# Sliding windows scattered from SBUF: whole first tiles of two neighbouring columns in place of half-filled ones

**Chip, cores, metric.** One core of a Trainium2 chip. The metric is the device time of one execution in microseconds, as a median over runs of the state "fast" (within 1.5% of the fastest run of the same kernel).

## The reference

```python
def setup_inputs():
    batch, c, h, w = (16, 64, 64, 64)          # float32, window 8, stride 4
def reference(x, window_size, stride):
    n_h = n_w = 15
    for i in range(n_h):
        for j in range(n_w):
            result[:, i, j] = x[:, :, 4*i:4*i+8, 4*j:4*j+8].copy()
```

Nothing is computed. 16.78 MB are read, each pixel goes into up to four windows, and 58.98 MB are written: 16 x 15 x 15 = 3600 output rows of 64 x 8 x 8 floats, 16 KB each.

## The kernel before

The input lies once in SBUF, as `L[128, 32, 16, 64]`. A partition is (channel half, batch, quarter of the height): 2 x 16 x 4. A store takes a tile `G[128, 64, 8, 8]`, one whole output row in each partition, and scatters it by a list of row numbers. ScalarE (ACT) and VectorE (DVE) copy the windows from `L` into one of four such tiles, GpSimd (POOL) issues the scatter. Rows whose number lies out of bounds (`FAR` is added) are skipped.

```python
    # loads: lower channels on SyncE's queue (28 of 32 channels) and POOL's (4), upper channels on POOL's
    for y in range(NY):                 # NY = 2 batch halves
        for q in range(HQ):             # HQ = 4 quarters of the height
            hw = y * HQ + q < HWP
            if hw:
                load(nc.sync, 0, y, q, SMALL, CL)
            load(nc.gpsimd, 0, y, q, 0, SMALL if hw else CL)
            load(nc.gpsimd, 1, y, q, 0, CL)
    # ... cut: fill() copies windows of 64 or 32 partitions from L into G
    EARLY = NG - 1                      # NG = 4 tiles
    zero = ipool.tile([P, 1], f32, name="zero")
    nc.vector.memset(zero[:, :], 0.0)
    for g in G:
        act(out=g.rearrange("p c r w -> p (c r w)"), in_=zero.to_broadcast([P, CFREE]))

    def part(y, j):                     # one column of one batch half: 64 of 128 rows, the others skipped
        g = tile_()
        for half in range(CH):
            fill(g, half, half, j, y * QP, QP, (dve, dve) if y and half else (act, dve))
        scatter(g, (idx_y0, idx_y1)[y], j, 0)

    def unit(j, s):
        g = tile_()
        if s == 0:                      # "plain": 128 rows, two ACT and two DVE copies
            for half in range(CH):
                fill(g, half, half, j, 0, HP, (act, dve))
            scatter(g, idx, j, s)
        else:                           # "crossed": 112 rows; 16 of one half are skipped, turn says which
            turn = int(crossed % 5 in (1, 3))
            crossed += 1
            fill(g, turn, s, j, 0, HP, (act, act))
            fill(g, 1 - turn, s + 1, j, 0, HP, (dve, dve))   # copy, and a stream shuffle for the lower rows
            scatter(g, (idx_hi, idx_lo)[turn], j, s)

    for j in range(EARLY):
        part(0, j)
    # ... cut: three times part(1, j) and a plain tile; then two crossed tiles and a plain one, and so on
    # the last column: two tiles, four stores each, on SyncE's queue
            free(nc.sync.dma_start(out=o_q[q * NSLOT + s, j], in_=g_q[QP + q : QP + q + (B - 1) * HQ + 1 : HQ]))
```

Parts exist because the first half of the batch is in SBUF long before the second (ACT's copies from the first half start at 29.52 us, the next ones, from the second, at 47.91): storing can be prepared while loads still run.

## Time and profile before

| | before |
|---|---|
| time, median | 194.81 us (194.69 to 195.04) |
| span in the profile | 192.9 us |
| DMA moved | 75.81 MB |
| busy: ACT, DVE, POOL | 72%, 57%, 28% |

How to read it: the bytes are fixed by the task, so the time is bytes over the rate of the DMA engines (420 GB/s from 58 to 180 us), plus every stretch in which those engines wait.

### The profile page before, as it was taken

Reading aid. Unit: us, or ns where it says so; the run is one execution under the profiler, and the core shown is the slowest. Engines: PE = TensorE matmul, PEld = TensorE weight load, DVE = VectorE, ACT = ScalarE, POOL = GpSimd, SP = SyncE. Lnnn points to the kernel's source line nnn. Section 1 sums busy time; section 2 is a strip of 40 time slices with the busy share of each in tenths; the row PEclk is TensorE's granted clock in tenths of the full one; section 3 lists DMA queues with packets and bytes.
Section 4 is the critical chain, followed back from the end, with each engine's and each line's share of the span. In section 5 each row is a group of like instructions: output and inputs, shape, how many; then the busy total and the mean of one; then the engine's idle time right before and its main releaser. Section 6 shows DMA issues by size and latency. Waiting matters only on the chain.

```text
span 192.9 us, 487 instructions
## 1 busy us (share of the span) xinstructions
DVE 110.2 (57%) x153; ACT 138.3 (72%) x70; POOL 54.6 (28%) x53
## 2 busy tenths in 40 slices
DVE  5000007700999979876876875874974794723330
ACT  8993008940897879999778777877977797754560
POOL 7402212531166430422214123134043124320000
DMA  2999999999989999999999999999999999999764
GB/s 79 337 404 400 399 401 397 401 401 407 421 357 418 404 423 421 425 421 404 426 425 428 420 411 418 432 435 411 404 435 418 425 431 404 418 432 435 321 292 177
DMA packets 11588, 75.81 MB, mean 393 GB/s; under 512 B 3888, under 2 KB 3888, under 8 KB 7984
## 3 DMA queue, kind: packets, MB, share of 16 engines
q0 software_dynamic: 9472, 66.34, 83.8%
q1 hardware_dynamic: 2112, 9.44, 12.4%
q14 instruction: 4, 0.03, 0.0%
HBM read 16.78 MB, written 69.21 MB: 446 GB/s over the span
## 4 chain that ended last, share of the span: by engine, by line
DMA 73%; DVE 12%; issue 7%; POOL 2%; ACTq 1%; ACT 1%; DVEq 0%; PEldq 0%
DMA out_dram<-G,idx 34%; DMA out_dram<-G,idx_hi 22%; DMA L<-in_x_dram 16%; DVE G L144 9%; POOL L L58 2%; DVE G L146 2%; DVE G L147 2%; ACTq L245 1%; ACT G L211 1%; DVEq L144 0%; POOL pi L69 0%; DVEq L146 0%; PEldq L245 0%; ACTq L211 0%
## 5 line engine op out<-in xcount | busy, mean ns | idle before, releaser
L144 ACT COPY G<-L 64x2048 f32<-64x2048 f32 (+1 forms) x61 | 115.3, 1896 | 40.0 <-issue 20.7
L144 DVE COPY G<-L 64x2048 f32<-64x2048 f32 (+1 forms) x37 | 45.0, 1224 | 41.9 <-DMA L<-in_x_dram 27.1
L147 DVE STREAM_SHUFFLE G<-L 64x1024 f32<-64x1024 f32 x30 | 38.3, 1277 | 0.0
L146 DVE COPY G<-L 64x1024 f32<-64x1024 f32 x30 | 21.6, 720 | 21.5 <-DMA out_dram<-G,idx 16.2
L124 POOL DMA_INDIRECT out_dram<-G,idx_hi x9 | 12.0, 1338 | 34.9 <-DVE G L147 24.5
L58 POOL DMA_DIRECT2D L<-in_x_dram x16 | 11.4, 715 | 23.9 <-DMA L<-in_x_dram 23.4
L124 POOL DMA_INDIRECT out_dram<-G,idx x11 | 12.4, 1126 | 18.6 <-ACT G L144 15.9
L124 POOL DMA_INDIRECT out_dram<-G,idx_lo x6 | 8.9, 1480 | 24.1 <-DVE G L147 17.0
L124 POOL DMA_INDIRECT out_dram<-G,idx_y x6 | 9.6, 1603 | 16.0 <-ACT G L144 8.9
L157 ACT COPY G<-zero 128x4096 f32<-128x4096 f32 x4 | 14.1, 3600 | 0.0
L211 ACT COPY G<-L 32x2048 f32<-32x2048 f32 x4 | 7.6, 1896 | 7.4 <-DMA out_dram<-G,idx 4.9
L211 DVE COPY G<-L 32x2048 f32<-32x2048 f32 x4 | 4.9, 1220 | 10.1 <-DMA out_dram<-G,idx 6.6
L157 ACT ACT_TABLE_LOAD x1 | 1.3, 1283 | 0.7 <-PEq L231 0.7
L155 DVE MEMSET zero<- 128x1 f32 x1 | 0.1, 59 | 0.8 <-PEq L231 0.8
L78 DVE CUSTOM_DVE_ANT_0 idx_y<-idx,th 128x2 uint16<-128x2 uint16 x2 | 0.3, 160 | 0.1
L78 DVE TENSOR_TENSOR th<-tc,tq 128x1 int32<-128x1 int32 x2 | 0.3, 158 | 0.1
L75 DVE TENSOR_SCALAR th<-tc 128x1 int32<-128x1 int32 x2 | 0.3, 154 | 0.0
L69 POOL IOTA pi<- 128x1 int32 x1 | 0.1, 125 | 0.4 <-PEq L245 0.4
L72 DVE TENSOR_SCALAR tb<-pi 128x1 int32<-128x1 int32 x1 | 0.2, 154 | 0.1
L147 DVE LOAD_MASK_SELECT G<-L x30 | 0.2, 6 | 0.0
L78 DVE CUSTOM_DVE_ANT_0 idx_hi<-idx,th 128x2 uint16<-128x2 uint16 x1 | 0.2, 160 | 0.0
L78 DVE CUSTOM_DVE_ANT_0 idx<-tb,th 128x2 uint16<-128x2 uint16 x1 | 0.2, 159 | 0.0
(16 smaller groups left out, 2.2 us busy)
## 6 DMA issues: line engine op xcount, KB each, us to landing
L<-in_x_dram POOLq DMA_DIRECT2D x8, 1024.0 KB, 21.0
L<-in_x_dram SPq DMA_DIRECT2D x8, 896.0 KB
out_dram<-G SPq DMA_DIRECT2D x8, 256.0 KB
L<-in_x_dram POOLq DMA_DIRECT2D x8, 128.0 KB, 21.1
out_dram<-G,idx POOLq DMA_INDIRECT x11, 14.5
out_dram<-G,idx_hi POOLq DMA_INDIRECT x9, 14.1
out_dram<-G,idx_y POOLq DMA_INDIRECT x6, 9.8
out_dram<-G,idx_lo POOLq DMA_INDIRECT x6, 12.9
```

The lines of the kernel that those rows point to most:

```text
L58: eng.dma_start(out=L[p0 : p0 + QP - HQ + 1 : HQ, c0:c1, :, :], in_=x_v[ch, y, q, :, c0:c1, :])
L69: nc.gpsimd.iota(pi[:, :], pattern=[[0, 1]], base=0, channel_multiplier=1)
L72: nc.vector.tensor_scalar(out=d[:, :], in0=pi[:, :], scalar1=shift, scalar2=mask, op0=ALU.logical_shift_right, op1=ALU.bitwise_and)
L75: nc.vector.tensor_scalar(out=d[:, :], in0=a[:, :], scalar1=float(m), scalar2=None, op0=ALU.mult)
L78: nc.vector.tensor_tensor(out=d[:, :], in0=a[:, :], in1=b[:, :], op=op)
L124: st = nc.gpsimd.indirect_dma_start(out=o_v, out_offset=bass.IndirectOffsetOnAxis(ap=ix[:, 0:1], axis=0), in_=g.rearrange("p c r w -> p (c ...
L144: copy(out=g[d, cs, :, :], in_=L[f, :, s * ST : s * ST + WS, cols])
L146: copy(out=g[d, cs, 0:ST, :], in_=L[f, :, s * ST : RB, cols])
L147: nc.vector.stream_shuffle(out=g[d, cs, ST:WS, :], in_=L[f, :, 0:ST, cols], mask=nxt)
L157: act(out=g.rearrange("p c r w -> p (c r w)"), in_=zero.to_broadcast([P, CFREE]))
L211: copy(out=g[d, ch * CL : (ch + 1) * CL, :, :], in_=L[f, :, s * ST : s * ST + WS, cols])
L245: with _tile.TileContext(nc) as tc:
```

## The change

Its intent: a part takes columns j and j + 1 of one batch half, so that all 128 rows are real; three plain tiles fewer are needed; no tile has unwritten rows, so the zeroing goes; the 16 skipped rows of the crossed tiles alternate between the halves; the last stores are issued on two queues. (The loads, four channels in each small one, are as they were.)

```diff
-    EARLY = NG - 1
-    zero = ipool.tile([P, 1], f32, name="zero")
-    nc.vector.memset(zero[:, :], 0.0)
-    for g in G:
-        act(out=g.rearrange("p c r w -> p (c r w)"), in_=zero.to_broadcast([P, CFREE]))
+    EARLY = 3
@@ def part(y, j):
-        for half in range(CH):
-            fill(g, half, half, j, y * QP, QP, (dve, dve) if y and half else (act, dve))
+        for d in range(P // QP):
+            s, dj = d // NY, d % NY
+            cols = slice((j + dj) * ST, (j + dj) * ST + WS)
+            for ch in range(CH):
+                f = (ch * NY + y) * QP
+                (act, dve)[(d + ch) % 2](
+                    out=g[d * QP : (d + 1) * QP, ch * CL : (ch + 1) * CL, :, :],
+                    in_=L[f : f + QP, :, s * ST : s * ST + WS, cols],
+                )
@@ def unit(j, s):
-            turn = int(crossed % 5 in (1, 3))
+            turn = crossed % 2
@@ order of the tiles
-        part(0, j)
+        part(0, 2 * n)
-    plain = [(j, 0) for j in range(EARLY, NW - 1)]
+    plain = [(j, 0) for j in range(2 * EARLY, NW - 1)]
-        for w in cross[:2]:
+        for w in cross[:3]:
@@ last column
-            free(nc.sync.dma_start(...))
+            free((nc.sync, nc.scalar)[s * q % 2].dma_start(...))
```

(Cut: the row numbers for the parts, which put the second column in place of the skipped rows.)

More of the change, by code (lines that the diff above doesn't have):

```diff
@@ L89 @@
     bits(th, 5, 1)
-    mul(th, th, FAR)
-    tt(idx_y0, idx, th, ALU.add)
-    nc.vector.tensor_scalar(out=th[:, :], in0=th[:, :], scalar1=-1.0, scalar2=FAR, op0=ALU.mult, op1=ALU.add)
-    tt(idx_y1, idx, th, ALU.add)
+    mul(idx_y0, th, 1 - YB * NWIN)
+    tt(idx_y0, idx_y0, idx, ALU.add)
+    nc.vector.tensor_scalar(out=idx_y1[:, :], in0=idx_y0[:, :], scalar1=float(YB * NWIN), scalar2=None, op0=ALU.add)
     nc.vector.tensor_scalar(out=tq[:, :], in0=tq[:, :], scalar1=float(HQ - 1), scalar2=FAR, op0=ALU.is_equal, op1=ALU.mult)
@@ L186, in unit @@
             scatter(g, (idx_hi, idx_lo)[turn], j, s)
-    for j in range(EARLY):
-        part(0, j)
-    plain = [(j, 0) for j in range(EARLY, NW - 1)]
+    for n in range(EARLY):
+        part(0, 2 * n)
+    plain = [(j, 0) for j in range(2 * EARLY, NW - 1)]
     cross = [(j, 2) for j in range(NW)]
-    for j in range(EARLY):
-        part(1, j)
+    for n in range(EARLY):
+        part(1, 2 * n)
         unit(*plain.pop(0))
     while plain:
-        for w in cross[:2]:
+        for w in cross[:3]:
             unit(*w)
-        cross = cross[2:]
+        cross = cross[3:]
         unit(*plain.pop(0))
@@ L213 @@
         for q in range(HQ):
-            free(nc.sync.dma_start(out=o_q[q * NSLOT + s, j], in_=g_q[QP + q : QP + q + (B - 1) * HQ + 1 : HQ]))
+            free((nc.sync, nc.scalar)[s * q % 2].dma_start(out=o_q[q * NSLOT + s, j], in_=g_q[QP + q : QP + q + (B - 1) * HQ + 1 : HQ]))
 _INS = ['x', 'window_size', 'stride']
```

## The prediction

> **What bounds the kernel now.** I read the page first: engine shares, the 40 slices, the DMA queues and the chain. Then I cut the span into windows at the dips of the DMA row, and read the timelines of ACT and POOL around each dip.
>
> ```profile
> DVE 110.2 (57%) x153; ACT 138.3 (72%) x70; POOL 54.6 (28%) x53
> ...
> DMA  2999999999989999999999999999999999999764
> ...
> DMA packets 11588, 75.81 MB, mean 393 GB/s; under 512 B 3888, under 2 KB 3888, under 8 KB 7984
> ...
> q0 software_dynamic: 9472, 66.34, 83.8%
> ...
> HBM read 16.78 MB, written 69.21 MB: 446 GB/s over the span
> ...
> DMA 73%; DVE 12%; issue 7%; POOL 2%; ACTq 1%; ACT 1%; DVEq 0%; PEldq 0%
> ```
>
> The 16 DMA engines are the bound: 9 in nearly every slice, 73% of the chain. 75.81 MB is exactly the input (16.78 MB) plus the output (58.98 MB) plus instructions. So **skipped rows move nothing**. The HBM line hides this: its 69.21 MB is the output plus 10.22 MB, which is 624 rows of 16 KB, just the number skipped (6 part stores x 64, 15 crossed stores x 16). That counter seems to count them; the packets do not: q0's 66.34 MB is 9.44 MB of loads and 3472 real rows. The packet records have 4-byte packets of about 9 ns in the skipped rows' places.
>
> ```profile
> core 0: us, DVE busy (x) ACT busy (x) POOL busy (x), PEclk, DMA share, GB/s
> ...
> 46.00:48.00 2.00, 0.02 (x1) 0.10 (x1) 0.00 (x0) 1.00 1.17 441
> 48.00:54.00 6.00, 5.88 (x5) 5.51 (x3) 1.52 (x1) 1.00 1.00 421
> 54.00:56.00 2.00, 1.94 (x3) 1.98 (x2) 1.36 (x2) 1.00 0.67 271
> 56.00:58.00 2.00, 1.94 (x3) 1.95 (x3) 0.84 (x1) 1.00 0.95 393
> 58.00:180.00 122.00, 88.10 (x115) 98.42 (x52) 35.17 (x27) 1.00 1.01 420
> 180.00:184.00 4.00, 1.39 (x2) 1.59 (x2) 0.00 (x0) 1.00 0.68 285
> 184.00:188.00 4.00, 1.05 (x1) 2.36 (x2) 0.00 (x0) 1.00 0.72 303
> 188.00:193.00 5.00, 0.00 (x0) 0.00 (x0) 0.00 (x0) 1.00 0.44 184
> ```
>
> From 48 to 54 us the stores in flight are part stores with half their rows skipped, and yet real bytes move at 421 GB/s, as later (420). From 420 GB/s over 16 engines, one 16 KB row costs an engine 0.624 us; a full store (8 rows an engine) 4.99 us, a crossed one on average 4.37 us. What is not full: the start; a dip at 54 to 58 us worth about 0.33 x 2 + 0.05 x 2 = 0.8 us; and the tail from 180 us, where the share is 0.7.
>
> ```profile
> 0.74 1.28 ACT L157 ACT_TABLE_LOAD   x1 [0.74 <-PEq L231]
> ...
> 29.52 11.01 ACT L144 COPY G<-L 32x2048 f32<-32x2048 f32 x6 [13.36 <-issue]
> 47.91 1.90 ACT L144 COPY G<-L 32x2048 f32<-32x2048 f32 x1 [7.37 <-issue]
> ...
> 52.48 1.86 POOL L124 DMA_INDIRECT out_dram<-G,idx_y  x1 [7.93 <-ACT G L144]
> ...
> 67.51 0.96 POOL L124 DMA_INDIRECT out_dram<-G,idx  x1 [0.65 <-ACT G L144]
> ...
> 180.19 8.72 SPq L214 DMA_DIRECT2D out_dram<-G  x8
> ...
> 182.57 3.81 ACT L211 COPY G<-L 32x2048 f32<-32x2048 f32 x2 [2.40 <-DMA out_dram<-G,idx_hi]
> ```
>
> The first lines show ACT free from 40.5 to 47.9 us: before, it is early. A POOL store issue takes 0.96 or 1.86 us.
>
> [...]
> 1. [...] 9 stores skip rows in the upper half and 6 in the lower, and after 180.2 us, when about half the engines have run out of scatter rows, the share is 0.68.
> 2. [...] 1.86 us at 52.5 us among VectorE copies, 0.96 us at 67.5 us beside a shuffle.
> 3. [...] The trace has 1283 ns and 1.90 us, for 32 and for 64 partitions.
> 4. [...] Here the last four issues on SP run from 186.41 to 188.91 us.
>
> **The change, part by part.**
>
> *Fewer skips.* Skipped rows fall from 624 to 240 and stores on POOL from 32 to 29 (6 parts, now full; 8 plain instead of 11; 15 crossed). Real rows stay 3600, so the DMA work is unchanged: worth about 0.
>
> *Balance.* Rows of engines 0-7, each: before, parts 6 x 4 = 24, plain 11 x 8 = 88, crossed 9 x 8 + 6 x 6 = 108, last column 8: 228 (engines 8-15: 222). After, 48 + 64 + (8 x 8 + 7 x 6 = 106) + 8 = 226 (the others 224). The longer half loses 2 rows: **-1.25 us**. Engines 0-7 are busy almost to the end, so this is on the path.
>
> *Zeroing gone.* ACT loses 14.1 us, all done by 16.2 us while it would wait for loads: 0. But the table load was issued with it at 0.74 us. In the built program of the changed kernel the table load stands just ahead of the first copy, behind waits for the loads. Loads of the first half land at 29.5 us, so ACT's first copy starts at 30.8.
>
> *More ACT work early.* A part tile had 1 or 2 copies on ACT, now 4 on each engine; ACT's cost per copy does not shrink with partitions. ACT for the first nine stores: 12 + 3 x (4 + 2) = 30 copies; before, 6 + 3 x (1 + 2) = 15. In program order, the lower-channel copies of three tiles come first. Unhindered pitch is 1.80 us (11.01 for six)[...]. Fills end at: tiles 1-3 at 45.4, 49.0, 52.6; tile 4 (second half's first part) 60.05; then plain 63.9, part 71.45, plain 75.3, part 82.8, plain 86.65.
>
> From fill end to the first packet before: POOL starts 0.3 us later, runs 0.96 or 1.86, packets begin 0.6 us after: 1.9 to 2.75 us. Loads leave the engines at about 46.9, as before. Stores, ready against engines free:
> - 1: ready 47.3, engines waited from 46.9: 0.4 lost; ends 52.3. 2 and 3 ready in time (52 and 55.4 at latest); end 57.3, 62.25.
> - 4: VectorE is filling tile 6, so 60.05 + 2.75 = 62.8: 0.55 lost; ends 67.8. 5 in time, ends 72.8.
> - 6: 71.45 + 2.75 = 74.2: 1.4 lost; ends 79.2. 7 in time, ends 84.2.
> - 8: 82.8 + 1.9 = 84.7 (VectorE shuffles by then): 0.5 lost; ends 89.7. 9 in time, ends 94.7.
>
> Sum 2.85 us, where the kernel before loses 0.8: **+2.05 us**, on all engines.
>
> *Three crossed in a row.* A crossed tile costs ACT 2 x 1.92 = 3.84 us and VectorE 2 x (0.69 + 1.28) = 3.95, both under 4.37 of DMA. With four buffers, landing to next packet (fill 4.0, issue 0.3 + 0.96 to 1.86, 0.6) is about 6.5 us against three stores (13 us) still queued: 0.
>
> *Issue of the last column on two queues.* The last four issues take 2.5 us in a row on SP; two and two take 1.25. But engines 0-7 have queued rows until about 188.6 and stand then only 0.2 to 0.3 us before the last rows reach them: **-0.3 us**, not 1.25.
>
> Sum: -1.25 + 2.05 - 0.3 = +0.5. 194.8 + 0.5 = **195.3 us**.
>
> **Rivals.**
> - *Skipped rows cost as much as real ones* (446 GB/s over the span would be the true rate): 384 fewer x 16 KB = 6.29 MB / 420 GB/s = 15 us, giving 180 us. For it: only the HBM line. Against it: 421 GB/s of real bytes in the window of half-skipped stores, and the byte sums. 2%.
> - *DMA-bound throughout, no starvation*: -1.25 - 0.3, and the old 0.8 us dip filled because the first three stores now queue 15 us, not 7.5: 192.5 us. For it: the deeper first queue, and that someone will have tried to balance this. Against it: ACT's 30 copies. 25%.
> - *ACT starves worse*: if every part issue meets VectorE's copies (+0.9 for store 8) and waits pitch the early copies at 1.92 (+1.3), 197 to 197.5. 15%.
> - *The tail binds at the last fill*: the last fill waits for the landing of the last crossed store, so the later stream delays it too; the saved 1.25 us of issue covers that. It gives the same sum within 0.5 us.
>
> **Range and chances.** Two opposing terms of 1 to 2 us decide. The size of starvation is uncertain by 1.5 us either way, the tail by 0.7. Together I take 193.3 to 197.2 for 8 in 10. Faster by 2% needs under 190.9, which even no starvation does not reach: 4%. Slower by 2% needs over 198.7, twice the starvation reckoned: 4%. Within 2%: 92%.
>
> **What would show each step right or wrong.** HBM written falls by 6.29 MB to 62.91 while DMA moves 75.8 MB still and the time stays. The ACT table load starts at about 29.5 us and the first copy at 30.8. ACT is nearly gapless from there to about 86 us. The DMA row is short of full at about 47, 62, 73 and 84 us, summing to some 3 us, and full from 95 to 180. In the tail, the halves of the engines run out of scatter rows closer together, about 1.2 us apart, not 5 to 7. I am wrong if the DMA row has no holes between 47 and 90 us (then 192.5), or if the span falls by the share of the skipped rows (then the packets hid a cost), or if holes appear among the crossed stores.

Passages that no trace or run of this case shows are cut: in the numbered list, its heading and the rules that stood ahead of what the trace had, and further down the cause that was given for the pitch of 1.92 us. No term of the sum is cut: it came to -1.25 + 2.05 - 0.3 = +0.5, and 194.8 + 0.5 = 195.3 us. What the steps around the cuts rest on:

- The balance. The traces number no engine: that the lower 64 rows of a store go to one half of the engines ("0-7") and the upper 64 to the other was the assumption. What was measured agrees with it within three rows an engine. The scatter rows in flight fall from 16 to 8 at 180.3 us; when the end of each row is followed to the next start in the packet records, eight chains have 211 to 214 scatter rows and eight have 220 to 223, where the count has 214 and 220 (228 and 222 less the 8 rows of the last column); after the change 214 or 215 and 218 to 220, where it has 216 and 218. Moving one store's skips from the upper half to the lower gave 1.2 us (b1_balance_only), against 1.25.
- The list's third item: 1283 ns is the table load, 1.90 us an ACT copy of 2048 elements a partition (mean 1897 ns in 64 partitions, 1894 in 32).
- The 1.92 us: six ACT copies in 11.51 us from 50.27 us on. That waits cause it is supposed in one of the rivals, and was not shown (run 9 speaks against it).
- The 1.25 us for two issues on each of two queues is an estimate, half of the 2.5 us of four issues on one.

## The result

| | before | after |
|---|---|---|
| time, median | 194.81 us (194.69 to 195.04, 4 runs) | 197.27 us (197.05 to 197.54, 4 runs) |
| ratio to before | | 1.0125 (95%: 1.0108 to 1.0143) |
| span in the profile | 192.9 us | 195.8 us |

A ratio here is the mean time of one kernel's fast runs over that of the other's fast runs of the same rounds, so not quite the ratio of the medians quoted.

The direction was foreseen, and the size was not: 2.5 us slower in place of 0.5, just above the upper end of the range (197.2). The page of the changed kernel, the lines that answer to those of before:

```profile
DMA  2999999998998896989999999999999999999983
...
DMA packets 11157, 75.81 MB, mean 387 GB/s; under 512 B 3457, under 2 KB 3457, under 8 KB 7553
...
q0 software_dynamic: 9040, 66.34, 82.5%
...
HBM read 16.78 MB, written 62.91 MB: 407 GB/s over the span
...
DMA 53%; issue 24%; POOL 10%; DVE 5%; ACT 3%; POOLq 0%; DVEq 0%; ACTq 0%; PEldq 0%
```

The HBM line's written bytes fell by 6.29 MB, which is the 384 skipped rows fewer; the bytes that the DMA engines moved did not change at all. The row of DMA digits now has a series of 8s and a 6 between slices 10 and 18 (about 44 to 88 us) where before it had one 8. DMA's share of the chain fell from 73% to 53%.

Next, windows of the changed kernel around those slices. The columns are the stretch, its length, busy time and number of instructions of each engine, the clock, the DMA share and the rate. (A DMA share can come out just above 1, because rows overlap in the records: 18 at once at 177 us of the kernel before.)

```profile
core 0: us, DVE busy (x) ACT busy (x) POOL busy (x), PEclk, DMA share, GB/s
44.00:48.00 4.00, 0.80 (x1) 3.95 (x3) 1.06 (x1) 1.00 0.84 282
48.00:60.00 12.00, 8.37 (x7) 11.83 (x8) 3.75 (x2) 1.00 0.99 415
60.00:64.00 4.00, 3.83 (x4) 3.95 (x3) 1.99 (x1) 1.00 0.77 328
...
72.00:76.00 4.00, 3.12 (x3) 3.95 (x3) 1.77 (x1) 1.00 0.76 322
...
84.00:88.00 4.00, 2.83 (x6) 3.95 (x3) 0.96 (x1) 1.00 0.86 360
```

ACT is busy to the last tenth in each (3.95 of 4.00, 11.83 of 12.00) while the rate falls to 282, 328, 322 and 360 GB/s. Four holes, at 47, 63, 74 and 86 us, near the places that the prediction listed (47, 62, 73 and 84). The whole stretch from 44 to 96 us, first before, then after the change:

```profile
44.00:96.00 52.00, 42.06 (x49) 43.43 (x23) 17.77 (x13) 1.00 1.00 411
...
44.00:96.00 52.00, 34.16 (x37) 51.34 (x28) 14.65 (x10) 1.00 0.92 380
```

Rate times length is 21.37 MB before and 19.76 MB after. The 1.6 MB missing are 3.8 us at 420 GB/s. That is where the time went.

Why ACT is behind shows in its timeline and in POOL's (start, length, engine, what, and what ended the idle time before):

```profile
29.80 1.28 ACT L166 ACT_TABLE_LOAD   x1 [29.80 <-DMA L<-in_x_dram]
...
31.10 30.64 ACT L166 COPY G<-L 32x2048 f32<-32x2048 f32 x16
...
46.68 1.06 POOL L123 DMA_INDIRECT out_dram<-G,idx_y  x1 [10.39 <-ACT G L166]
...
62.02 2.01 POOL L123 DMA_INDIRECT out_dram<-G,idx_y  x1 [5.50 <-ACT G L166]
```

The table load waits for the loads now, and 16 copies follow without a gap: 30.64 us, a pitch (from the start of one copy to the start of the next) of 1.92 us. POOL has waited for ACT at every part (10.4 us, 5.5 us). Before, the first three scatters were issued at 37 to 44 us, well ahead of the end of the loads at 47; now the first is issued at 46.7. The first and the third of the kernel before:

```profile
37.23 2.08 POOL L124 DMA_INDIRECT out_dram<-G,idx_y  x1 [1.01 <-ACT G L144]
...
43.59 0.96 POOL L124 DMA_INDIRECT out_dram<-G,idx_y  x1 [0.43 <-issue]
```

The tail is better than before, as balance should make it:

```profile
184.00:188.00 4.00, 2.44 (x2) 2.92 (x2) 0.00 (x0) 1.00 0.90 373
188.00:192.00 4.00, 0.00 (x0) 0.88 (x1) 0.00 (x0) 1.00 0.85 356
192.00:196.00 4.00, 0.00 (x0) 0.00 (x0) 0.00 (x0) 1.00 0.18 74
```

Before, the DMA share is 0.68 from 180 to 184 us, 0.72 from 184 to 188 and 0.44 from there to the end at 192.9; now it is 0.90 from 184 to 188, 0.85 from 188 to 192 and 0.18 in the rest. In the packet records the scatter rows in flight fall from 16 to 8 at 180.3 us before and at 185.8 now, and most of the rest end some 5 us later before, some 2 us later now. The two halves of the engines end closer together.

### The profile page after: what moved, and what is told of

Read it like the earlier page. It is cut to its first block, busy times and chain, and to the rows that moved or that the text cites. A ratio compares the mean times of both kernels' runs of the same rounds, so it can differ in the third digit from the quotient of the medians.

```text
span 195.8 us, 482 instructions
## 1 busy us (share of the span) xinstructions
DVE 113.0 (58%) x154; ACT 141.5 (72%) x75; POOL 48.4 (25%) x50
## 2 busy tenths in 40 slices
DMA packets 11157, 75.81 MB, mean 387 GB/s; under 512 B 3457, under 2 KB 3457, under 8 KB 7553
## 3 DMA queue, kind: packets, MB, share of 16 engines
q1 hardware_dynamic: 2048, 8.91, 11.7%
HBM read 16.78 MB, written 62.91 MB: 407 GB/s over the span
## 4 chain that ended last, share of the span: by engine, by line
DMA 53%; issue 24%; POOL 10%; DVE 5%; ACT 3%; POOLq 0%; DVEq 0%; ACTq 0%; PEldq 0%
DMA out_dram<-G,idx_hi 27%; DMA L<-in_x_dram 12%; POOL out_dram L123 8%; DMA out_dram<-G,idx 7%; DMA out_dram<-G,idx_lo 7%; DVE G L166 4%; POOL L L58 2%; ACT G L212 2%; ACT G L143 1%; DVE G L146 1%; DVE G L145 0%; POOLq L123 0%; DVEq L166 0%; POOL pi L69 0%; DVEq L145 0%
## 5 line engine op out<-in xcount | busy, mean ns | idle before, releaser
L143 ACT COPY G<-L 64x2048 f32<-64x2048 f32 x46 | 87.1, 1896 | 9.8 <-DMA out_dram<-G,idx_hi 4.7
L166 DVE COPY G<-L 32x2048 f32<-32x2048 f32 x24 | 29.3, 1221 | 36.4 <-DMA L<-in_x_dram 26.2
L166 ACT COPY G<-L 32x2048 f32<-32x2048 f32 x24 | 45.5, 1896 | 0.5
L145 DVE COPY G<-L 64x1024 f32<-64x1024 f32 x30 | 20.7, 689 | 19.1 <-DMA out_dram<-G,idx_hi 10.4
L143 DVE COPY G<-L 64x2048 f32<-64x2048 f32 x16 | 19.7, 1231 | 7.8 <-DMA out_dram<-G,idx 6.7
L166 ACT ACT_TABLE_LOAD x1 | 1.3, 1283 | 29.8 <-DMA L<-in_x_dram 29.8
L123 POOL DMA_INDIRECT out_dram<-G,idx_hi x8 | 9.9, 1237 | 23.3 <-ACT G L143 20.4
L123 POOL DMA_INDIRECT out_dram<-G,idx x8 | 9.7, 1218 | 20.5 <-ACT G L143 17.7
L123 POOL DMA_INDIRECT out_dram<-G,idx_lo x7 | 8.0, 1138 | 24.8 <-DVE G L146 17.4
L212 ACT COPY G<-L 32x2048 f32<-32x2048 f32 x4 | 7.6, 1896 | 7.2 <-DMA out_dram<-G,idx_lo 5.0
L212 DVE COPY G<-L 32x2048 f32<-32x2048 f32 x4 | 4.9, 1220 | 9.9 <-DMA out_dram<-G,idx_lo 6.3
```

The lines of the kernel that those rows point to most:

```text
L123: st = nc.gpsimd.indirect_dma_start(out=o_v, out_offset=bass.IndirectOffsetOnAxis(ap=ix[:, 0:1], axis=0), in_=g.rearrange("p c r w -> p (c ...
L143: copy(out=g[d, cs, :, :], in_=L[f, :, s * ST : s * ST + WS, cols])
L145: copy(out=g[d, cs, 0:ST, :], in_=L[f, :, s * ST : RB, cols])
L166: (act, dve)[(d + ch) % 2](out=g[d * QP : (d + 1) * QP, ch * CL : (ch + 1) * CL, :, :], in_=L[f : f + QP, :, s * ST : s * ST + WS, cols],)
L212: copy(out=g[d, ch * CL : (ch + 1) * CL, :, :], in_=L[f, :, s * ST : s * ST + WS, cols])
```

## The experiments

My theory: the first nine stores are starved by ACT, at 1.9 us a copy, and nothing else of weight is new. Rivals: buffers or POOL's issue make the holes; skipped rows cost something after all; the tail sets the end.

**1. The table load early** (changed kernel)

```diff
+    warm = ipool.tile([P, 2], f32, name="warm")
+    nc.vector.memset(warm[:, 0:1], 0.0)
+    act(out=warm[:, 1:2], in_=warm[:, 0:1])
     EARLY = 3
```

> The changed kernel with one tiny ScalarE copy at the start, so that the table load runs at about 0.7 us and not at 29.8. Theory (ScalarE's chain of copies starves the DMA engines in the first nine stores): the whole chain starts 1.28 us sooner, the hole at 47 us closes, and the store stream up to 95 us ends 1.28 us sooner: 197.3 - 1.3 = 196.0 us. Rival (the holes come from buffers that land late or from GpSimd's issue time): the later holes grow by what the first loses, 197.3 us.

Measured: 196.16 us, ratio 1.0061 (1.0046 to 1.0077): 1.1 us less than the changed kernel, near the length of one table load (1.28 us). The 16 copies start at 29.81 instead of 31.10 us.

```profile
0.74 1.28 ACT L153 ACT_TABLE_LOAD   x1 [0.74 <-PEq L235]
...
29.81 30.64 ACT L169 COPY G<-L 32x2048 f32<-32x2048 f32 x16 [27.59 <-DMA L<-in_x_dram]
```

The hole at 47 us is closed (401 GB/s from 44 to 48 us). The holes at 62 and 74 us are deeper than in the changed kernel (262 and 264 GB/s), the one at 86 is shallower (393), and the whole stretch from 44 to 96 us gains. So ACT's chain of copies is on the path; had late buffers or POOL's issue time alone made the holes, the time should have stayed at 197.3 us.

**2. Three copies of a part on ACT, five on DVE** (changed kernel, table load still late)

```diff
-                (act, dve)[(d + ch) % 2](
+                (act, dve)[int((d + ch) % 2 or d == 3)](
```

> The changed kernel with three of a part's eight copies on ScalarE and five on VectorE, the table load still late. Theory: ScalarE spends 5 x 1.92 = 9.6 us on a part and a plain tile, under the 9.98 us of their DMA, the holes at 47, 63, 74 and 86 us (4.7 us together) close: 192.6 us. Rival (GpSimd's issue time beside VectorE's copies makes the holes): more VectorE copies make them worse, 197.3 us or more. Rival (the gain of full tiles is in the steady stage and something there is lost): no change.

Measured: 191.98 us, ratio 0.9853 (0.9838 to 0.9868). One copy in eight moved, and 5.3 us went. The windows of this kernel, over the four holes:

```profile
44.00:48.00 4.00, 3.92 (x4) 4.00 (x3) 2.77 (x2) 1.00 1.09 387
...
60.00:64.00 4.00, 3.89 (x5) 3.95 (x3) 0.29 (x1) 1.00 1.00 416
...
72.00:76.00 4.00, 3.89 (x5) 3.95 (x3) 0.64 (x1) 1.00 1.07 455
...
84.00:88.00 4.00, 2.97 (x5) 2.93 (x3) 0.48 (x1) 1.00 0.97 406
```

The holes are closed, although POOL's issues beside DVE's copies are as long as ever (1.84 to 2.21 us each for the second to fifth). So it was ACT's share of the copies, and POOL's issue time alone made no hole.

**3. The balance undone** (changed kernel)

```diff
-            turn = crossed % 2
+            turn = int(crossed % 5 in (1, 3))
```

> The changed kernel with the old turn (three upper skips to two lower). Theory: engines 0 to 7 carry 228 rows again and not 226, the end comes 1.25 us later: 198.5 us, and the longer half runs out of rows later than the other by 5 or 6 rows. Rival (balance of rows is hidden by the wait for the last fill): under 0.3 us of change.

Measured: 198.62 us, ratio 1.0198 (1.0184 to 1.0211): 1.35 us more than the changed kernel, against 1.25 worked out from two rows of 0.624 us. The rows of the longer half are on the path.

**4. The skipped rows put back** (changed kernel)

```diff
+    far = itile("far")                  # every row number out of bounds
+    nc.vector.tensor_scalar(out=far[:, :], in0=idx[:, :], scalar1=FAR, scalar2=None, op0=ALU.add)
     while plain:
+        if len(plain) <= 3:
+            scatter(L.rearrange(...)[:, 0:CFREE].rearrange(...), far, 0, 0)
```

> The changed kernel with three more scatters among the crossed stores whose 128 rows all lie out of bounds, so that 624 rows are skipped again, as before. Theory (a skipped row moves nothing): written bytes of the HBM line go back to 69.21 MB, DMA moves 75.81 MB still, time 197.3 + 0.0 to 0.4 us. Rival (a skipped row costs as much as a real one): 384 x 16 KB at 420 GB/s is 15 us, 212 us.

Measured: 197.94 us, ratio 1.0163 (1.0148 to 1.0179): 0.7 us more than the changed kernel for 384 skipped rows and three more issues, not 15 us.

```profile
DMA packets 11588, 75.81 MB, mean 387 GB/s; under 512 B 3888, under 2 KB 3888, under 8 KB 7984
...
HBM read 16.78 MB, written 69.21 MB: 438 GB/s over the span
```

The HBM line counts the skipped rows again, the moved bytes stay, and the small packets rise by 431, that is one for each of the 384 rows and 16 more for each of the three scatters (one packet aside). The 0.7 us is above the 0.4 I allowed. Some 0.3 us of it are slower rows (in the packet records 0.6252 us each instead of 0.6238, times 217 rows an engine); the rest stays unsplit. Skipping 384 rows is thus worth 0.7 us at most.

**5. The old last column** (changed kernel), **and the new turn and the last column alone** (kernel before)

```diff
@@ e5_tail_undone (changed kernel)
-            free((nc.sync, nc.scalar)[s * q % 2].dma_start(...))
+            free(nc.sync.dma_start(...))
@@ b1_balance_only (kernel before)
-            turn = int(crossed % 5 in (1, 3))
+            turn = crossed % 2
@@ b2_balance_tail (kernel before): as b1, and
-            free(nc.sync.dma_start(...))
+            free((nc.sync, nc.scalar)[s * q % 2].dma_start(...))
```

> The changed kernel with all eight stores of the last column on SyncE's queue again. Theory: 0.3 us more, 197.6 us. Rival (the end hangs on the last fill, and the issues after it): 1.2 us more, 198.5 us.

> The kernel before with the new turn alone (8 upper skips, 7 lower). Theory (engines 0 to 7 carry 226 rows instead of 228 and are on the path to the end): 1.25 us less, 193.5 us. Rival (the last fill and its issue set the end, not the rows): under 0.4 us.

> The kernel before with the new turn and the last column's stores on two queues. Theory: with the rows on the path, another 0.3 us at most, 193.3 us; everything that the change gives without its full tiles. If it comes out within 1 us of the changed kernel with the 3 to 5 split (191.98 us), full tiles are worth no more than the old hole at 54 to 58 us.

Measured: e5_tail_undone 197.12 us, ratio 1.0112 (1.0097 to 1.0128), the same as with two queues (1.0125) within the intervals. b1_balance_only 193.68 us, ratio 0.9943 (0.9929 to 0.9956): 1.2 us gained, as reckoned. b2_balance_tail 194.08 us, ratio 0.9964 (0.9950 to 0.9978): with the second queue 0.4 us slower, not 0.3 faster. So the second queue gives nothing, and of these two parts of the change the balance alone gives something. b2_balance_tail is 2.1 us above the split of run 2 (191.98), so full first tiles are worth more than the old dip of 0.8 us.

**6. Both edits: early table load and the split of 3 to 5** (changed kernel)

> The changed kernel with the early table load and the 3 to 5 split. Theory (after the split alone no hole is left for the table load to widen): as the split alone, 191.9 us, within 0.3 us. Rival (ScalarE still delays the stream somewhere): up to 1.3 us less.

Measured: 190.69 us, ratio 0.9795 (0.9782 to 0.9809). My theory was wrong here: the early table load still gives 1.3 us, though the split alone had left no hole. What differs is the rate while the engines are full. In the DMA packets of the trace (counted in the records, not in a view) a 16 KB row takes 0.6163 us on average in this kernel, and 0.6238 in the changed kernel and in the split alone; from 52 to 94 us it is 0.611 to 0.613 here, and 0.619 to 0.628 in the split alone. The windows of this kernel stand under run 8.

**7. One queue for the last column, on top of both edits; and no skipped turn of the buffers**

```diff
@@ e10_both_one_queue: run 6, and the last column as in the kernel before
@@ e7_both_no_gap: run 6, and
     j = NW - 1
-    tile_()
```

> The kernel with both edits and all eight last stores on SyncE's queue. From the two earlier pairs (changed kernel: 0.15 us less with one queue; kernel before with the new turn: 0.4 us less): 190.3 to 190.7 us. If the issues of the last fill bind here, 191.5 us.

> The kernel with both edits, and the last column's two tiles in the next two buffers (the skipped turn taken out), so that their fills wait for stores that land about 4 us sooner. Theory (the engines of the longer half are busy to the end, the other half is idle 3 to 4 us): the idle of the tail shrinks, 190.7 less 0.3 to 1.0 us. Rival (rows alone set the end): no change; or slower by up to 1 us, where the early stores on the hardware queues hold back the last crossed stores.

Measured: e10_both_one_queue 190.74 us, ratio 0.9789 (0.9775 to 0.9802), as run 6. e7_both_no_gap 191.66 us, ratio 0.9840 (0.9827 to 0.9854): 1.0 us slower. Filling the last two tiles sooner costs time; the rival that said so was right on the sign, and why was not looked into.

**8. One hole on purpose** (run 6, and the first tile delayed)

```diff
         scatter(g, (idx_y0, idx_y1)[y], j, 0)     # and ahead of it, for y == 0 and j == 0:
+            for again in range(2):
+                act(out=g[2 * QP : 3 * QP, 0:CL, :, :], in_=L[0:QP, :, ST : ST + WS, 0:WS])
```

> The kernel with early table load and 3 to 5 split (190.69 us), with two needless repeats of one ScalarE copy in the first tile, so that the first store is ready at about 49 us, some 2 us after the loads leave the engines. Theory A (a hole costs itself and then slower rows, because the 16 engines start again in step): the rows take 0.62 us and more afterwards instead of 0.611 to 0.617, and the time is 190.7 + 2.0 + 1.2 to 1.7 = 193.9 to 194.4 us. Theory B (row time has nothing to do with the hole; what was seen in the kernel with both edits is another cause): rows stay at 0.611 to 0.617 us, 192.7 us.

Measured: 194.34 us, ratio 0.9984 (0.9971 to 0.9998): 3.65 us more than run 6, for one hole. Windows of run 6 (both edits):

```profile
44.00:50.00 6.00, 5.88 (x6) 4.54 (x4) 3.45 (x3) 1.00 1.07 411
50.00:100.00 50.00, 40.90 (x46) 44.51 (x24) 15.64 (x11) 1.00 1.01 430
100.00:176.00 76.00, 54.67 (x77) 60.20 (x33) 18.52 (x16) 1.00 1.01 425
```

and of run 8 (the same with one hole):

```profile
44.00:50.00 6.00, 5.88 (x6) 5.95 (x5) 3.05 (x2) 1.00 0.76 274
50.00:100.00 50.00, 38.20 (x41) 44.03 (x24) 17.58 (x12) 1.00 1.01 422
100.00:176.00 76.00, 54.72 (x80) 60.26 (x32) 18.41 (x16) 1.00 1.01 421
```

The hole itself is (411 - 274) x 6 = 0.82 MB, 2.0 us at 420 GB/s. After it the DMA share is the same 1.01, and yet the rate is 422 and 421 instead of 430 and 425: 8 x 50 + 4 x 76 = 0.70 MB, another 1.7 us. The sum, 3.6 us, is what was measured. So **in this kernel a hole costs itself and then a slower rate**, and theory A of the expectation stands in its numbers. Run 6 and both runs of experiment 7, all without the hole and on two chips, have 0.611 to 0.614 us a row up to 94 us. In the packet records the 16 engines start rows at moments spread over nearly a whole row's time (0.61 us) where the rate is 430, and after a hole all 16 start within about 0.2 us of each other. That the starting in step is the cause of the slower rows is argued from this, and not shown by itself. The split alone (run 2) has 422 and 421 GB/s in the same two windows without a hole to be seen. Its first store was ready only at 46.8 us, so that 11 of its first 16 rows start within 0.2 us (in run 6 within 0.5 us): a few engines had waited. That so short a wait is enough is a guess which no run tests.

The kernel before has this loss too: its rows take 0.611 us from 46 to 52 us, and 0.620 to 0.632 after its one dip at 54 us.

**9. Copies ordered by partitions** (changed kernel, one look)

```diff
-    for n in range(EARLY):
-        part(0, 2 * n)
+    gs = [tile_() for n in range(EARLY)]
+    for d in range(P // QP):
+        for ch in range(CH):
+            for n, g in enumerate(gs):
+                ...  # the copy of block (d, ch) into g, as in part()
+    for n, g in enumerate(gs):
+        scatter(g, idx_y0, 2 * n, 0)
```

> The changed kernel with the copies of its first three tiles in the order of blocks, the three tiles inside, so that three ScalarE copies in a row have the same source and destination partitions. If copies overlap where partitions stay the same: two of three pitches are 1.80 us and every third 1.92, and the twelve end at about 31.1 + 8 x 1.80 + 3 x 1.92 + 1.90 = 53.2 us, not 54.1 (but the first tile is complete only at the tenth copy, so the hole at 47 us is 3 us wider and the time above 199 us). If something else sets the pitch: 1.92 throughout.

Measured, state unknown: 198.26 us. The line of ACT:

```profile
30.88 22.03 ACT L196 COPY G<-L 32x2048 f32<-32x2048 f32 x12
```

Twelve copies in 22.03 us, against 11 x 1.92 + 1.90 = 23.0 at the pitch of the changed kernel. Single starts in the trace are 1.80 us apart (30.88, 32.69, 34.49) within three equal blocks, and 1.90 to 1.92 where the block changes. The last three ACT copies of run 2's first tiles, which have equal partitions too, are also 1.80 us apart. So in these traces the pitch was 1.80 us where a copy keeps the partitions of the one before, and 1.90 to 1.92 us where it changes them. (The time was under my 199 us: the hole at the end of the loads was wider, but the later holes were nearly gone.)

## Why the prediction was right or wrong

- **Skipped rows are worth nothing: right.** Fewer skips changed no moved byte, and 384 skips put back cost 0.7 us at most (run 4), not 15. The rival that read 446 GB/s as the true rate is out.
- **Balance, -1.25 us: right.** 1.35 us in the changed kernel (run 3), 1.2 us in the kernel before (b1_balance_only).
- **The table load moves onto the path: right,** 1.28 us at 29.8 us; taking it off gives 1.1 us (run 1).
- **ACT's 30 copies starve the DMA engines at stores 1, 4, 6 and 8: right in mechanism and place.** The holes lie at 47, 63, 74 and 86 us, and moving one ACT copy in eight closes them (run 2).
- **The size of that term was wrong, and this is the step that failed:** "Unhindered pitch is 1.80 us (11.01 for six)". The prediction said +2.05 us against before; the bytes missing from 44 to 96 us say 3.8, which is 1.75 more. I took 1.80 from six copies of the kernel before that fall into two groups of equal partitions. In the changed kernel neighbouring copies change partitions, and all 16 follow each other at 1.91 to 1.92. Run 9 shows both pitches in one kernel. Over the 16 copies ahead of the fourth store that is nearly 1.4 us of the lateness (fill end 61.74 instead of 60.05; the loads landed 0.3 us later as well); by the eighth store's fill it is 84.78 instead of 82.8. All of it falls on holes, because there ACT is the bound. The rival "ACT starves worse" (15%, 197 to 197.5 us) had the right number, half by luck: it put the early copies at 1.92 us, but for waits and not for partitions, and its other half, 0.9 us more for store 8, did not come (that issue took 0.96 us).
- **The tail, -0.3 us: wrong.** A second queue gives nothing (run 5, e5_tail_undone; run 7, e10_both_one_queue) or costs 0.4 us (b2_balance_tail).
- **The sum** with measured terms is -1.2 (balance) + 3.8 (holes) + 0 (tail) = 2.6 us, and 2.5 was measured. The slower rate after a hole did not enter the difference, since both kernels have holes early: 0.6239 and 0.6238 us a row. It entered what a repair is worth: the rival "no starvation" was put at 192.5 us, and with the holes gone and the engines never dry the kernel takes 190.69, because the rows then take 0.6163 us: 217 scatter rows an engine x 0.0075 = 1.6 us.

The fastest kernel found is the changed one with both edits: 190.69 us, 2.05% under the kernel before, with the interval of the ratio at 0.9782 to 0.9809, so that it is not settled whether the gain is a full 2%. Its gain over b1_balance_only, 3.0 us, is what whole first tiles, the early table load and the split give together: no dip, and no slow rows up to 94 us. No run separates their shares.

## What to carry to other kernels

When the DMA engines are the bound, count moved bytes (here 75.81 MB before and after), not counters that include skipped ones (69.21 and 62.91 MB written); then ask of each stage which engine fills the next tile, and price it with the pitch of the very sequence that it will run, not with one of another shape. An idle prologue hides things that become costly when it is removed: here a table load of 1.28 us that rode on a needless zeroing (taking it off the path again gave 1.1 us, run 1). A small hole at the start of a long stream cost nearly twice here (run 8: 2.0 us of hole and 1.7 us of slower rate), so it is worth a try to have the first store ready before the loads end.
